# Hybrid conformer block: first gate pair's weight sums in the conv's spare buffers, token sums reordered, conv results in three places, fillers in two more attention slots

## The chip, the cores and the metric

The kernel runs on one core of one Trainium2 chip. The metric is the device time of one execution in microseconds; lower is better. Three runs of the kernel before took 1736.94, 1739.24 and 1739.51 us, a median of 1739.24.

## The reference

One transformer block over 1024 tokens with 1024 channels. `h @ w_in` gives five things: the two halves of a gated conv input, q, k and v for 16 heads, and the logits of two gates.

```python
h = rms_norm(x, norm1_g[l])
z = h @ w_in[l]
glu_in, q, k, v, gate_logits = jnp.split(z, SPLITS, axis=-1)
a = a_val * jax.nn.sigmoid(a_gate)
a = causal_depthwise_conv(a, conv_w[l], conv_b[l])      # width 31
a = jax.nn.silu(rms_norm(a, conv_norm_g[l]))
y_a = a @ w_conv_out[l]
...                                                     # dilated window attention, three groups
y_b = o @ w_attn_out[l]
g_a, g_b = jnp.split(jax.nn.sigmoid(gate_logits + gate_b[l]), 2, axis=-1)
x = x + (g_a * y_a + g_b * y_b) @ w_out[l]
h = rms_norm(x, norm2_g[l])
u = causal_depthwise_conv(h @ w_up[l], ffn_conv_w[l], ffn_conv_b[l])
x = x + (jax.nn.silu(u_gate) * u_val) @ w_down[l]
```

## The kernel before

All products run in fp32r with both operands split into a high part, rounded on ScalarE (ACT), and a low part, the difference, on VectorE (DVE). Three matmuls (high x high, high x low, low x high) make one product. `split` does the rounding and the difference; `wsplit` puts the two parts of a weight into the buffers `whi` and `wlo` (four each), and `stage` loads a weight or an activation block into one of four `raw` buffers of 128 x 1024 through the SP queue. Who wants a fifth `raw` buffer waits until the first is read for the last time.

The order of the stages: normed input; gated conv input; q, k, v; the gates; attention; the two output products; the feed-forward part. The 31-tap conv (`conv_branch`, L558) runs on VectorE beside the q, k, v products; its buffers are `cacc`, two of `codd` (513 columns), one `csum` (527 columns).

**The gate stage** computes 16 blocks of 128 gate channels for all 1024 tokens. Blocks 10 and 11 are plain products (`side_steps`, printed as `gate`). Ten others are done in five pairs (`PAIRS`, n = 0 to 4) by a Strassen-Winograd scheme: seven half-size products instead of eight. It needs sums of weight quarters (`sums`: s1 = g0 + g1, s2 = s1 - v0, s3 = v0 - g0, s4 = v1 - s2, four VectorE instructions of 128 x 512 on the pair's two raw weights v and g, with one more raw buffer for s1 and s2) and sums of token blocks. The token sums are made once, in `token_forms(i)` for i = 0 and 1, each for two of four k-blocks: it loads r22, r12, r11 into raw buffers and r21 into the place of its own result, forms three differences, and splits them into b12, t1 and t2; a fourth, t4, follows in the returned function `fourth`. The results lie in the pool `phT`, where the operands of the attention come later.

For each pair the loop (L805 on) runs the products in this order: X with s12 and t2, Y with s12 and t1, X with s3 and b12, then for n = 1 to 3 the first product of the next pair (`gx`), then X with s3 and t4 and Y with s4 (for n = 0 and 4 the other way round). Here X and Y are accumulators in PSUM; ScalarE and VectorE take them out as c11, c12, p5 and c21, which go to DRAM. `parts(n, which, name)` splits a weight sum, `load(n, which)` loads a weight.

**Interleaved with it:** `conv_factors` (n = 0) sums the conv's squares by matmul and takes the root on GpSimd; `conv_spread` (n = 1) builds a diagonal on VectorE and spreads it over the partitions by 16 matmuls (`psr`); `conv_result(c)` for c = 0 to 7 scales channel block c on VectorE, applies SiLU on ScalarE and stores it from ScalarE's queue. Blocks 0 to 3 stand in n = 1, 4 to 7 in n = 2, each time ahead of the b12 product.

**What sets the order.** Inside `tc.manual_schedule(engines=hand)` the instructions of ScalarE, VectorE and TensorE are issued as written. Everything else, such as the conv and all loads on the SP queue, is placed by a planner that works with estimated times; what is written earlier goes first where both could go. `tc.issue_after(ins)` keeps a block behind one instruction of the same engine. Each queue then runs in that fixed order.

**The attention** is a hand-ordered loop over 128 slots (head, half, query block): `score`, then `fill(front)`, the transposes `flip` of the slot five before, the weighted sums, `powers`, `share` and `fill(behind)`. `share` scales the probabilities on GpSimd. `fill(k)` takes k steps of three matmuls from the remaining plain gates and the conv's output product; `FRONT` and `BEHIND` give the numbers for the eight slots of a head. What is left of these steps runs after the last slot.

Of the kernel before, what the change touches and what calls it, by code (L numbers as in the profile page):

```python
# [13 lines left out]
F32 = mybir.dt.float32  # L14
F32R = mybir.dt.float32r
# [6 lines left out]
P = 128  # L22
# [13 lines left out]
FRONT = (1, 1, 0, 0, 0, 1, 0, 1)  # L36
BEHIND = (1, 1, 1, 1, 0, 1, 1, 0)
# [3 lines left out]
PAIRS = ((0, 1), (2, 3), (4, 5), (6, 7), (8, 9))  # L41
# [15 lines left out]
def block_kernel(ctx: ExitStack, tc: tile.TileContext, x, xT, x0, g2, pack, mask,  # L57
# [22 lines left out]
    def split(hi, lo, src):  # L80

        act.activation(hi, src, AF.Copy)  # L82
        dve.tensor_tensor(out=lo, in0=src, in1=hi.bitcast(F32), op=ALU.subtract)  # L83
# [216 lines left out]
    if True:  # L300
# [385 lines left out]
        def token_forms(i):  # L686
            ks = slice(2 * i, 2 * i + 2)
            view = lambda t: t.rearrange("p (a b) -> p a b", a=2)
            load = lambda n, k, half: stage(dh[:, k + 2 * i : k + 2 * i + 2, half * 512 : half * 512 + 512], f"h{n}_{i}")
            r22, r12, r11 = (view(load(n, k, half)) for n, k, half in (("22", 4, 1), ("12", 0, 1), ("11", 0, 0)))  # L690
            r21 = form["t4"][1][:, ks]
            sp.dma_start(r21.bitcast(F32), dh[:, 4 + 2 * i : 6 + 2 * i, 0:512])
            tt = lambda o, a, b, op: dve.tensor_tensor(out=o, in0=a, in1=b, op=op)
            tt(r11, r12, r11, sub)
            tt(r12, r22, r12, sub)
            tt(r22, r22, r11, sub)

            def rounded(dst, src):
                split(dst[0][:, ks], dst[1][:, ks], src)

            rounded(b12, r12)
            rounded(form["t1"], r11)
            rounded(form["t2"], r22)

            def fourth():
                tt(r22, r21.bitcast(F32), r22, sub)
                rounded(form["t4"], r22)

            return fourth

        def conv_factors():
            pss = bank_ps("pss")
# [47 lines left out]
        def load(n, which):  # L760
            raws[n][which] = stage(w_ch[16 + PAIRS[n][which]], f"g{which}_{n}")

        def sums(n):
            v, g = raws[n][0], raws[n][1]
            s = raws[n][2] = wp.tile([P, 1024], F32, tag="raw", bufs=4, name=f"gs_{n}")
            tt_(s[:, 0:512], g[:, 0:512], g[:, 512:], add)
            tt_(s[:, 512:], s[:, 0:512], v[:, 0:512], sub)
            tt_(g[:, 0:512], v[:, 0:512], g[:, 0:512], sub)
            tt_(v[:, 512:], v[:, 512:], s[:, 512:], sub)

        def parts(n, which, name):
            src = raws[n][which] if which != "s4" else raws[n][0][:, 512:]
            pw[n][name] = [four(t) for t in wsplit(src, f"{name}_{n}")]

        ENG = mybir.EngineType
        hand = {ENG.Activation, ENG.DVE, ENG.PE}
        with tc.manual_schedule(engines=hand):
            fourths = [token_forms(i) for i in range(2)]
            load(0, 0)
            load(0, 1)  # L780
            fourths[0]()
            sums(0)
            parts(0, 2, "s12")
            fourths[1]()
            parts(0, 1, "s3")
        with tc.issue_after(settled1.ins):
            conv_acc = conv_branch()
        cover(16 * len(PLAIN) - COVER)
        for _ in early_gates:
            pass  # L790
# [9 lines left out]
        with tc.manual_schedule(engines=hand):  # L800
            for n in range(2):
                xz[n] = gate_first(n, firsts[n])
                begun(n)
            load(1, 0)
            for n, (a, b) in enumerate(PAIRS):  # L805
                X = xz[n][:, 0:512]
                Y = bank_ps(f"gy_{n}")
                (sh, sl), (gh, gl) = pw[n]["s12"], pw[n]["s3"]
                inner = 0 < n < N - 1
                if n + 2 < N:  # L810
                    load(n + 2, 0)
                if n == 3:
                    p1_cm.__exit__(None, None, None)
                    p2_cm = tc.tile_pool(name="ph2", bufs=1, reuse_waits="tile")
                    p2 = p2_cm.__enter__()
                    pool2.append(p2)
                if n + 1 < N:
                    load(n + 1, 1)
                if n == 3:
                    tiles[0] = head(0)  # L820
                parts(n, "s4", "s4")
                if inner:
                    parts(n + 1, 0, "v")
                product(X, sh[:, 4:8], sl[:, 4:8], *form["t2"], False)
                c12 = quarter(f"c12_{n}")
                act.activation(c12, X, AF.Copy)
                product(Y, sh[:, 0:4], sl[:, 0:4], *form["t1"], True)
                p5 = quarter(f"p5_{n}")
                act.activation(p5, Y, AF.Copy)
                if n == 0:  # L830
                    rs8 = conv_factors()
                if n == 1:
                    conv_spread(rs8)
                if 0 < n < 3:
                    for c in range(4 * n - 4, 4 * n):
                        conv_result(c)
                product(X, gh[:, 0:4], gl[:, 0:4], *b12, False)
                tt_(p5, X, p5, add)
                sp.dma_start(dgate[b][:, 512:1024], p5)
                if n + 1 < N:  # L840
                    sums(n + 1)
                if inner:
                    xz[n + 1] = big_ps(f"gx_{n + 1}")
                    for i in range(2):
                        product(xz[n + 1][:, i * 512 : i * 512 + 512], *(t[:, 4 * i : 4 * i + 4] for t in pw[n + 1]["v"]),
                                *left[i], True)
                    parts(n + 1, 2, "s12")
                    begun(n + 1)
                else:
                    product(Y, *pw[n]["s4"], *b22, False)  # L850
                    tt_(c12, Y, c12, add)
                    if n + 1 < N:
                        parts(n + 1, 2, "s12")
                product(X, gh[:, 4:8], gl[:, 4:8], *form["t4"], False)
                c21 = quarter(f"c21_{n}")
                act.activation(c21, X, AF.Copy)
                sp.dma_start(dgate[b][:, 0:512], c21)
                if inner:
                    product(Y, *pw[n]["s4"], *b22, False)
# [12 lines left out]
    if True:  # L872
# [102 lines left out]
        with tc.manual_schedule(engines={ENG.Activation, ENG.DVE, ENG.PE}):  # L975
            pend = []
            fill(1)
            for at in range(len(slots) + BACK + 1):
                count[2] += 1
                cur = slots[at] if at < len(slots) else None  # L980
                front, behind = (FRONT[at % 8], BEHIND[at % 8] + (at == 4)) if cur else (2, 2)
                if cur is not None:
                    h, half, n = cur
                    if (half, n) == (0, 2) and h + 1 < H:
# [661 lines left out]
```

## Time and profile before

| what | value |
|---|---|
| median of three runs | 1739.24 us |
| profiled execution, whole | 1738.48 us |
| profiled execution, span from first to last instruction | 1736.5 us |
| granted TensorE clock over the span | 0.999 |
| TensorE busy | 99% of the span |
| VectorE busy | 77% of the span |
| ScalarE busy | 47% of the span |
| GpSimd busy | 10% of the span |

How to read the rows of the profile: PE is TensorE (PEld its weight loads), DVE VectorE, ACT ScalarE, POOL GpSimd, SP the queue that issues most transfers. Rows in order of time give the start in us from the span's start, the duration, the engine, the line of the kernel, the operation, what is written and read, and in brackets the idle time of that engine just before, with what ended it. Rows of waits give the engine and line that waited, what it waited for, the total, the number of times and the longest. The chain of waits is the work that ended last, followed back step by step.

### The profile page before, as it was taken

To read this page: it belongs to the slowest core of one execution; us is meant where nothing else is said; L and a number is where in the kernel's file an instruction comes from. 1 tells how busy PE (TensorE), PEld (TensorE's weight loads), DVE (VectorE), ACT (ScalarE), POOL (GpSimd) and SP (SyncE) were. 2 spreads that over 40 slices of the span, in tenths; PEclk is the share of its full clock that TensorE was granted. 3 is DMA by queue.
4 is the path that set the end of the run, shared out by engine and by line. 5 is a ranking of instruction groups with operands and counts; after the bars stand their busy time and mean duration, and the time that the engine had idled before them with its cause. 6 is when DMAs were issued, how large, how long until landed. Compare 5 with 4: busy or idle time off the path is not lost.

```text
span 1736.5 us, 22876 instructions
## 1 busy us (share of the span) xinstructions
PE 1725.9 (99%) x8147; PEld 1437.9 (83%) x8147; DVE 1333.1 (77%) x2032; ACT 810.7 (47%) x1284; POOL 178.6 (10%) x188
## 2 busy tenths in 40 slices
PE   9999999999999999999999999999999999999999
PEld 7888888888878888888888888888888888888887
DVE  5999999999776567867757663787777776789863
ACT  5421233233345577777765442555445444533431
POOL 0000232132000133332220000000000000000000
PEclk9999999999999999999999999999999999999999
DMA  9311145345537967877639585622221222398851
GB/s 375 139 53 49 51 140 170 109 134 176 180 122 240 291 185 216 238 216 201 198 122 338 206 296 203 225 107 85 86 85 73 85 85 85 128 370 307 292 176 49
DMA packets 159842, 299.02 MB, mean 172 GB/s; under 512 B 13296, under 2 KB 63088, under 8 KB 159216
## 3 DMA queue, kind: packets, MB, share of 16 engines
q1 hardware_dynamic: 157280, 291.14, 50.5%
q10 hardware_dynamic: 2448, 6.42, 0.9%
q8 instruction: 64, 1.05, 0.2%
q14 instruction: 50, 0.41, 0.1%
HBM read 213.62 MB, written 83.89 MB: 171 GB/s over the span
## 4 chain that ended last, share of the span: by engine, by line
PE 96%; DVE 1%; DMA 1%; issue 0%; ACT 0%; POOL 0%; SPq 0%; ACTq 0%; DVEq 0%; POOLq 0%
PE dx L1458 7%; PE xz L138 6%; PE xz L139 6%; PE xz L140 6%; PE dy L1458 5%; PE qkv L131 5%; PE qkv L133 5%; PE qkv L132 5%; PE pp L913 4%; PE y L138 2%; PE y L139 2%; PE y L140 2%; PE o L928 2%; PE o L927 2%; PE s L894 2%; PE s L893 2%
## 5 line engine op out<-in xcount | busy, mean ns | idle before, releaser
L131 PE MATMUL qkv<-hi_qkv,hT 128*128 128x512 f32 x384 | 151.2, 395 | 0.0
L133 PE MATMUL qkv<-hi_qkv,hT 128*128 128x512 f32 x384 | 149.8, 391 | 0.0
L132 PE MATMUL qkv<-lo_qkv,hT 128*128 128x512 f32 x384 | 149.8, 391 | 0.0
L83 DVE TENSOR_TENSOR pl<-pp,ph 128x512 fp32r<-128x512 f32 (+2 forms) x191 | 99.7, 550 | 42.4 <-ACT ph L82 42.0
L82 ACT ACTIVATE ph<-pp 128x512 fp32r<-128x512 f32 (+2 forms) x191 | 86.6, 489 | 74.0 <-PE pp L913 72.1
L898 DVE CUSTOM_DVE_ANT_0 p<-s,m 128x128 f32<-128x128 f32 (+3 forms) x120 | 90.5, 754 | 39.6 <-PE pp L913 22.0
L1361 DVE SCALAR_TENSOR_TENSOR u<-u,pk 128x1023 f32<-128x1023 f32 x88 | 112.4, 1279 | 1.2 <-ACT u L1359 0.9
L907 POOL TENSOR_SCALAR p<-p,st 128x128 f32<-128x128 f32 (+3 forms) x120 | 90.6, 756 | 206.0 <-DVE st L906 179.1
L107 POOL TENSOR_TENSOR rs<-ss,mhalf 128x8 f32<-128x8 f32 x32 | 69.5, 2175 | 291.4 <-DVE ss L106 291.3
L903 ACT ACTIVATE p<-p,st 128x128 f32<-128x128 f32 (+3 forms) x120 | 93.6, 780 | 8.2 <-DVE st L898 5.5
L580 DVE SCALAR_TENSOR_TENSOR cacc<-csum,both,cacc 128x512 f32<-128x512 f32 x120 | 90.0, 750 | 0.3
L580 DVE SCALAR_TENSOR_TENSOR cacc<-apad,pk,cacc 128x512 f32<-128x512 f32 x120 | 88.9, 751 | 0.0
L83 DVE TENSOR_TENSOR lo_uv<-raw_uv,hi_uv 128x1024 fp32r<-128x1024 f32 x20 | 24.5, 1226 | 79.9 <-ACT hi_uv L82 79.9
L580 DVE SCALAR_TENSOR_TENSOR codd<-apad,pk,codd 128x513 f32<-128x513 f32 x112 | 84.5, 755 | 0.7 <-ACT codd L573 0.7
L133 PEld LDWEIGHTS qkv<-hi_qkv,hT 128*128 128x128 f32 x384 | 72.1, 188 | 15.1
L132 PEld LDWEIGHTS qkv<-lo_qkv,hT 128*128 128x128 f32 x384 | 72.2, 188 | 14.2
L131 PEld LDWEIGHTS qkv<-hi_qkv,hT 128*128 128x128 f32 x384 | 72.1, 188 | 14.2
L913 PE MATMUL pp<-ident,p 128*128 128x128 f32 x540 | 79.8, 273 | 1.5 <-POOL p L907 1.4
L913 PEld LDWEIGHTS pp<-ident,p 128*128 128x128 f32 x540 | 64.1, 140 | 13.9 <-POOL p L907 2.4
L927 PE MATMUL o<-ph,v 128*128 128x512 f32 (+2 forms) x191 | 74.1, 392 | 0.0
L138 PE MATMUL xz<-blk_t,hi_s3g 128*128 128x512 f32 x176 | 68.7, 390 | 0.0
L138 PE MATMUL xz<-h2left,hi_uv 128*128 128x512 f32 x176 | 68.6, 390 | 0.0
(429 smaller groups left out, 4962.9 us busy)
## 6 DMA issues: line engine op xcount, KB each, us to landing
wr<-w_down SPq DMA_DIRECT2D x45, 512.0 KB, 5.5
gr<-dff SPq DMA_DIRECT2D x62, 256.0 KB, 5.0
raw_qkv<-w_qkv SPq DMA_DIRECT2D x24, 512.0 KB, 3.9
dff<-u SPq DMA_DIRECT2D x22, 512.0 KB, 2.6
raw_uv<-w_up SPq DMA_DIRECT2D x21, 512.0 KB, 3.2
raw_ug<-w_up SPq DMA_DIRECT2D x20, 512.0 KB, 3.2
raw_g<-w_ch SPq DMA_DIRECT2D x16, 512.0 KB, 4.0
dv<-v SPq DMA_DIRECT2D x16, 512.0 KB, 3.3
```

Source lines behind the costliest of these rows:

```text
L83: dve.tensor_tensor(out=lo, in0=src, in1=hi.bitcast(F32), op=ALU.subtract)
L131: pe.matmul(ps, ah, hi[:, k % 2, :], start=(k == 0), stop=False)
L132: pe.matmul(ps, ah, lo[:, k % 2, :], start=False, stop=False)
L133: pe.matmul(ps, al, hi[:, k % 2, :], start=False, stop=(k == KT - 1))
L138: pe.matmul(o, wh[:, k, :], bh[:, k, :], start=(start and k == 0), stop=False, skip_group_check=not start)
L139: pe.matmul(o, wh[:, k, :], bl[:, k, :], start=False, stop=False, skip_group_check=not start)
L140: end = pe.matmul(o, wl[:, k, :], bh[:, k, :], start=False, stop=(k == 3), skip_group_check=not start)
L580: dve.scalar_tensor_tensor(out=out_, in0=src[:, i : i + size], scalar=w(i), in1=out_, op0=ALU.mult, op1=ALU.add)
L913: pe.transpose(pp[:, qb * P : (qb + 1) * P], pts[qb][:, kt * P : (kt + 1) * P], ident)
L927: pe.matmul(o[:, c], v[:, kt, :], ph[:, c], start=(kt == 0), stop=False)
L1361: dve.scalar_tensor_tensor(out=acc[:, d:], in0=src[:, : T - d], scalar=w(2 - d), in1=acc[:, d:], op0=ALU.mult, op1=ALU.add)
L1458: pe.matmul(banks[n][:, cols], a[:, c], b[:, d], start=(start and i == 0 and m == 0), stop=(stop and i == nf - 1 and m == 2), skip_group_c ...
```

## The change

Five edits.

1. `token_forms` returns its three splits as functions, in the order t1, t2, b12, fourth, instead of running b12, t1, t2 at once. Step 0 runs b12, t1, t2 and its fourth. Step 1 runs t2, then the pair's weight sums and the split of s12, then t1, b12 and the split of s3. Its fourth moves into the pair loop, behind the split of s4 for n = 0.
2. The first pair's second weight is not loaded into a raw buffer but, in two halves of 256 KB, into the conv's `csum` buffer and into 512 new columns in the token pool. Its sums s1 and s2 go to the two `codd` buffers. `sums` and `parts` work on halves, so the splits of s12 and s3 of the first pair take two instructions of 512 columns on each engine instead of one of 1024.
3. `conv_branch` is written ahead of the token forms instead of behind them.
4. `conv_spread` moves behind the b12 product of n = 1. The conv's results 0 and 1 move to the end of n = 1, 2 to 5 stand in n = 2 ahead of the b12 product, 6 and 7 at the end of n = 2.
5. In slots 2 and 3 of the attention one more step is filled in (slot 4 already had one more).

```diff
             def rounded(dst, src):
-                split(dst[0][:, ks], dst[1][:, ks], src)
-
-            rounded(b12, r12)
-            rounded(form["t1"], r11)
-            rounded(form["t2"], r22)
+                return lambda: split(dst[0][:, ks], dst[1][:, ks], src)
 
             def fourth():
                 tt(r22, r21.bitcast(F32), r22, sub)
-                rounded(form["t4"], r22)
-
-            return fourth
+                rounded(form["t4"], r22)()
+
+            return rounded(form["t1"], r11), rounded(form["t2"], r22), rounded(b12, r12), fourth
...
         def sums(n):
-            v, g = raws[n][0], raws[n][1]
-            s = raws[n][2] = wp.tile([P, 1024], F32, tag="raw", bufs=4, name=f"gs_{n}")
-            tt_(s[:, 0:512], g[:, 0:512], g[:, 512:], add)
-            tt_(s[:, 512:], s[:, 0:512], v[:, 0:512], sub)
-            tt_(g[:, 0:512], v[:, 0:512], g[:, 0:512], sub)
-            tt_(v[:, 512:], v[:, 512:], s[:, 512:], sub)
+            (v0, v1), (g0, g1) = halves(raws[n][0]), halves(raws[n][1])
+            if 2 not in raws[n]:
+                raws[n][2] = wp.tile([P, 1024], F32, tag="raw", bufs=4, name=f"gs_{n}")
+            s0, s1 = halves(raws[n][2])
+            tt_(s0, g0, g1, add)
+            tt_(s1, s0, v0, sub)
+            tt_(g0, v0, g0, sub)
+            tt_(v1, v1, s1, sub)
...
         def parts(n, which, name):
-            src = raws[n][which] if which != "s4" else raws[n][0][:, 512:]
-            pw[n][name] = [four(t) for t in wsplit(src, f"{name}_{n}")]
+            src = raws[n][which] if which != "s4" else halves(raws[n][0])[1]
+            if isinstance(src, list):
+                hi, lo = (wp.tile([P, 1024], F32R, tag=f"w{a}", bufs=4, name=f"{a}_{name}_{n}") for a in ("hi", "lo"))
+                for c, t in zip(HALVES, src):
+                    split(hi[:, c], lo[:, c], t)
+                pw[n][name] = [four(t) for t in (hi, lo)]
+            else:
+                pw[n][name] = [four(t) for t in wsplit(src, f"{name}_{n}")]
...
+        with tc.issue_after(settled1.ins):
+            conv_acc = conv_branch()
+        raws[0][1] = [p1.tile([P, 527], F32, tag="csum", bufs=1, name="g1_0a")[:, 0:512], pT.tile([P, 512], F32, name="g1_0b")]
+        raws[0][2] = [p1.tile([P, 513], F32, tag="codd", bufs=2, name=f"gs_0{a}")[:, 0:512] for a in "ab"]
+        for i, t in enumerate(raws[0][1]):
+            sp.dma_start(four(t), w_ch[16 + PAIRS[0][1]][:, 4 * i : 4 * i + 4])
         with tc.manual_schedule(engines=hand):
-            fourths = [token_forms(i) for i in range(2)]
+            forms0 = token_forms(0)
+            for k in (2, 0, 1, 3):
+                forms0[k]()
+            first, second, third, fourth = token_forms(1)
             load(0, 0)
-            load(0, 1)
-            fourths[0]()
+            second()
             sums(0)
             parts(0, 2, "s12")
-            fourths[1]()
+            first()
+            third()
             parts(0, 1, "s3")
-        with tc.issue_after(settled1.ins):
-            conv_acc = conv_branch()
...
                 parts(n, "s4", "s4")
+                if n == 0:
+                    fourth()
...
+                if n == 2:
+                    for c in (2, 3, 4, 5):
+                        conv_result(c)
+                product(X, gh[:, 0:4], gl[:, 0:4], *b12, False)
                 if n == 1:
                     conv_spread(rs8)
-                if 0 < n < 3:
-                    for c in range(4 * n - 4, 4 * n):
-                        conv_result(c)
-                product(X, gh[:, 0:4], gl[:, 0:4], *b12, False)
...
                     begun(n + 1)
+                    for c in {1: (0, 1), 2: (6, 7)}.get(n, ()):
+                        conv_result(c)
...
-                front, behind = (FRONT[at % 8], BEHIND[at % 8] + (at == 4)) if cur else (2, 2)
+                front, behind = (FRONT[at % 8], BEHIND[at % 8] + (at in (2, 3, 4))) if cur else (2, 2)
```

More of the change, by code (lines that the diff above doesn't have):

```diff
@@ L761, in load, with halves @@
             raws[n][which] = stage(w_ch[16 + PAIRS[n][which]], f"g{which}_{n}")
+        def halves(t):
+            return t if isinstance(t, list) else [t[:, 0:512], t[:, 512:]]
         def sums(n):
-            v, g = raws[n][0], raws[n][1]
-            s = raws[n][2] = wp.tile([P, 1024], F32, tag="raw", bufs=4, name=f"gs_{n}")
-            tt_(s[:, 0:512], g[:, 0:512], g[:, 512:], add)
-            tt_(s[:, 512:], s[:, 0:512], v[:, 0:512], sub)
-            tt_(g[:, 0:512], v[:, 0:512], g[:, 0:512], sub)
```

## The prediction

> **What bounds the kernel now.** I read the page first, then the list of waits of the matmul engine, then that engine in order of time, and then the chain of work around the one long wait.
>
> ```profile
> span 1736.5 us, 22876 instructions
> PE 1725.9 (99%) x8147; PEld 1437.9 (83%) x8147; DVE 1333.1 (77%) x2032; ACT 810.7 (47%) x1284; POOL 178.6 (10%) x188
> ```
>
> TensorE is busy for 1725.9 of 1736.5 us, and no matmul is added or removed by the change. So it can win only where TensorE stands or runs slowly. Its waits, over the whole span (total, times, longest):
>
> ```profile
> PE gx L138 <- ACT hi_s L82: 2.2, 1, 2.2
> ...
> PE pp L913 <- POOL p_first L907: 0.7, 1, 0.7
> PE gx L140 <- DVE lo_s L83: 0.5, 1, 0.5
> PE psr L727 <- DVE dgs L722: 0.3, 1, 0.3
> ```
>
> The change aims at these four: the two of gx (first gate pair), psr (the conv's factors spread) and p_first (the attention's first flip). The first pair's place in order of time (start, duration, what it waited for):
>
> ```profile
> 478.97 0.39 PE L138 MATMUL gx<-hT,hi_gw 128*128 128x512 f32 x1
> ...
> 489.62 0.39 PE L140 MATMUL gx<-hT,lo_gw 128*128 128x512 f32 x1
> 492.25 0.50 PE L138 MATMUL gx<-gt,hi_s 128*128 128x512 f32 x1 [2.25 <-ACT hi_s L82]
> ...
> 493.51 0.80 PE L140 MATMUL gx<-gt,lo_s 128*128 128x512 f32 x1 [0.53 <-DVE lo_s L83]
> 494.11 0.63 PE L138 MATMUL gx<-gt,hi_s 128*128 128x512 f32 x1
> 494.53 0.63 PE L139 MATMUL gx<-gt,hi_s 128*128 128x512 f32 x1
> ...
> 497.24 0.39 PE L138 MATMUL gy<-gt,hi_s 128*128 128x512 f32 x1
> ```
>
> From 478.97 to 489.62 lie 47 steps: one matmul every 0.2266 us. After 489.62, 13 steps lead to the first gy at 497.24. At that pace it would start at 489.62 + 13 x 0.2266 = 492.57. So this place costs 4.67 us, of which only 2.78 is shown as idle: after the wait the matmuls come every 0.42 us (494.11 to 494.53), and the clock row says why (columns: length, busy time of PE, PEld, DVE, ACT and POOL, granted clock, DMA share, GB/s):
>
> ```profile
> 490.00:500.00 10.00, 7.23 (x27) 5.57 (x26) 8.12 (x10) 4.67 (x6) 0.00 (x0) 0.83 0.47 171
> ```
>
> [...]
>
> **What makes it late.** The chain of waits before it:
>
> ```profile
> 464.76 5.80 DMA gt<-dh
> 470.56 1.22 DVE hT L83
> 471.77 1.14 DVE gt L83
> 472.94 5.49 DMA raw_h<-dh
> 478.55 1.24 DVE raw_h L693
> ...
> 485.70 1.14 DVE raw_h L693
> ...
> 486.87 1.07 ACT gt L82
> ...
> 489.70 0.69 DVE gs L758
> ...
> 491.11 1.20 DVE raw_g L758 x2
> ```
>
> and the loads on the SP queue, with a row of the page for how long such a weight load takes to land (4.0 us):
>
> ```profile
> 455.31 4.02 SPq L87 DMA_DIRECT2D raw_h<-dh  x3
> ...
> 471.80 1.49 SPq L87 DMA_DIRECT2D raw_h<-dh  x2
> ...
> 483.45 0.34 SPq L87 DMA_DIRECT2D raw_g<-w_ch  x1
> ```
> ```profile
> raw_g<-w_ch SPq DMA_DIRECT2D x16, 512.0 KB, 4.0
> ```
>
> Only four raw buffers exist. The token blocks of step 0 hold them until 471.8, those of step 1 follow, and the pair's weight loads get a buffer only from 483.45 on. The second lands near 489, the four weight sums run from 489.70, and TensorE's second wait, for the low half of their split, ends at 493.51. TensorE wanted it at 489.85.
>
> **The change, part by part.**
>
> **The first pair's second weight and its sums leave the raw buffers.** They go into the conv's csum and codd buffers and 2 KB of the token pool, so its load can be issued as soon as the conv's last squares are added, which the trace has at:
>
> ```profile
> 468.21 0.69 DVE L591 TENSOR_TENSOR sqacc<-sqacc,csum 128x512 f32<-128x512 f32 x1
> ```
>
> It lands by about 468.9 + 4 = 473. The first weight needs the raw buffer of step 0's r22, which the new order frees early: `fourth` of step 0 (now 485.70: a subtraction of 1.14, a copy of 1.07 on ACT and a split of 1.14, some 3.4 us) comes straight after the third split of step 0, in VectorE's idle time ahead of 478.55, where step 1's blocks land. The three splits of step 0 end at 470.56 + 3 x 1.14 = 474.0, so it ends at about 477.4, and the weight lands at 477.4 + 4.0 = 481.4. The blocks of step 1 still arrive at 478.4, since their buffers come free at the same two splits. Then VectorE does, in the new order: three block sums of 1.24 to 482.2; the t2 split (ACT 1.07, then 1.14) to 484.5; four weight sums of 0.60 to 486.9; the s12 split in two halves of 0.6 to 488.1. **So TensorE finds both operands 1.7 us before 489.85.** Next it needs t1 (at 489.85 + 12 x 0.2266 = 492.57; split ends 489.3), then b12 and s3 (after gy and the conv's sum of squares, past 496; ends 490.4 and 491.6), then the step-1 `fourth`, moved behind s4, past 500 (ends 495.6). None is late. All of the 4.67 us is counted, for the clock never falls if TensorE never stands. From below: if the step-1 blocks and weights land 3 us later, which is a doubling of half their flight, 1.3 us of wait stay, and with the slow steps behind them some 2.
>
> The conv is now traced ahead of the token forms, so its last six VectorE instructions may go before them instead of between them. That is 0 to 2.4 us (four at 0.6) earlier for the forms, since VectorE waits for step 0's blocks anyway. I take 0.
>
> **The next deadline.** Behind this stands the second pair's split:
>
> ```profile
> 508.53 1.22 DVE L83 TENSOR_TENSOR lo_s<-gs,hi_s 128x1024 fp32r<-128x1024 f32 x1
> ```
> ```profile
> 509.96 0.39 PE L138 MATMUL gx<-gt,hi_s 128*128 128x512 f32 x1
> ```
>
> It ends at 509.75, 0.2 us before it is read. It starts from TensorE's own product b12, so it moves with TensorE, as long as its weights are there. These take raw buffers freed by t1, b12 and s4 of the first pair (489.3 to 492.2), land by 496.2 and are needed near 499.9. I take 0; if they kept their old times, this would give back 1 to 2 us.
>
> **The spread of the conv's factors** goes behind the product b12. It costs TensorE the step from 515.17 to 515.89, of 0.72 instead of 0.23: 0.49 us.
>
> ```profile
> 515.17 0.39 PE L140 MATMUL gy<-gt,lo_s 128*128 128x512 f32 x1
> 515.89 2.05 PE L727 MATMUL psr<-dgs,ones 128*128 128x128 f32 x16 [0.33 <-DVE dgs L722]
> ```
>
> With 12 matmuls (2.72 us) between, the diagonals are done before TensorE asks: all 0.49 us is won. The p5 sum and the third pair's sums queue behind the two copies of psr on VectorE, but four conv products (4.6 us) no longer stand before them, so they come earlier.
>
> **The conv's results** keep their eight products and eight SiLUs. Two go to the end of n=1, four stay in n=2, two go to the end of n=2. The last two come ahead of the s3 split of the fourth pair:
>
> ```profile
> 518.71 4.63 DVE L733 TENSOR_TENSOR cacc<-cacc,sqacc 128x1024 f32<-128x1024 f32 x4
> ```
> ```profile
> 549.52 1.23 DVE L83 TENSOR_TENSOR lo_s<-raw_g,hi_s 128x1024 fp32r<-128x1024 f32 x1 [2.46 <-ACT hi_s L82]
> ```
> ```profile
> 555.91 0.39 PE L138 MATMUL gx<-hT,hi_s 128*128 128x512 f32 x1
> ```
>
> Two products of 1.16 and two SiLUs, taken by the ACT row of that size above, 1.07, push that split by 4.5 us at most, if nothing overlaps: from 550.75 to 555.2. It is read at 555.91: covered, and taken as 0.
>
> **Two more fillers** (the sum over slots 2, 3, 4 is three; slot 4 had one already). Each is three matmuls, 0.68 us, moved from the attention's end to its start. The place they fill:
>
> ```profile
> 592.57 0.49 PE L913 MATMUL pp<-ident,p_first 128*128 128x128 f32 x3
> 593.75 0.33 PE L913 MATMUL pp<-ident,p_first 128*128 128x128 f32 x1 [0.70 <-POOL p_first L907]
> ```
> ```profile
> 592.65 1.05 POOL L907 TENSOR_SCALAR p_first<-p_first,st 128x512 f32<-128x512 f32 x1 [0.46 <-DVE st L906]
> ```
>
> GpSimd's share ends at 593.70; its chain hangs on VectorE and ACT, not on the fillers. TensorE comes 1.36 us later to the flip, past 593.70: the 0.70 us is won. At the end two steps fewer cover the first weights of the next stage:
>
> ```profile
> 920.93 3.49 DVE L83 TENSOR_TENSOR lo_ao<-raw_ao,hi_ao 128x1024 fp32r<-128x1024 f32 x3
> ```
> ```profile
> 922.82 0.39 PE L114 MATMUL yb<-oT,hi_ao 128*128 128x512 f32 x1
> ```
>
> The first of the three is done at 922.1; the first yb would stand at 921.46 and read it two steps later, 921.9. I charge 0.3 us (0 to 0.7).
>
> **Sum:** 4.67 + 0.49 + 0.70 - 0.30 = 5.56 us. The profiled execution took 1738.48 us (span 1736.5 and 2.0 around it): 1732.9. The median of the runs, 1739.24, stands 0.76 above it: **1733.7 us**. Its own range is 1732.2 to 1735.5.
>
> **The rivals.**
>
> *Half of it comes back.* The freed time meets the next deadlines: late weights of the second pair (1 to 2 us), or a rest of the wait in the first (2 us). For it: 0.2 us of margin at 509.75. Against it: all loads are triggered earlier. 5.56 - 2.5 = 3.1 won: 1736.2.
>
> *The loads of the first pair block the SP queue.* SP's rows come one after another, so one that waits holds those behind it. If the csum load is placed ahead of the three raw_h loads at 455.31, these wait for the conv's release at 468.9 instead. They then land at about 475, step 0 (three sums, three splits, the fourth: 10.3 us) ends at 485.8; step 1's blocks, freed at 480 to 481, land at 486.8; and the chain worked out above (9.6 us from there) ends at 496.1. TensorE stands 6.25 us instead of 2.78, and with the same 1.9 us of slow steps the place costs 8.15: 3.5 more than now, less 0.9 from the other parts: 1741.8, slower. The three loads are issued by 455.31 + 4.02 = 459.3 now and the chain has 1.7 us to spare, so it decides from about 461 on, and each further microsecond costs one. For it: the load is traced first. Against it: a load is placed when its buffer is expected free, and VectorE's order has that behind the first block sum, which itself needs those three loads.
>
> *The change doesn't do what it says.* The instructions of the conv and the forms land on VectorE in another order than traced, the s12 split stays near 493, and only psr and p_first are won: 1739.24 - 0.9 = 1738.3.
>
> **How the numbers follow.** Forecast 0.60; half back 0.17; blocked queue 0.13; not as said 0.10. A measurement of this kernel tells about 0.2% from no change, 3.5 us: faster means under 1735.8, slower over 1742.7. The forecast is faster nearly throughout (0.58), half back in four tenths of its cases (0.07); the blocked queue is slower by that much where it is held past 470 (0.07, and 0.03 for a mishap of it elsewhere). Faster 0.65, same 0.25, slower 0.10. The range runs from 1731.8 (the forms 2.4 us earlier bring nothing, but the attention's start up to 1 us more, and no charge at its end) to 1740.0, which holds all but the blocked queue.
>
> **What would show it.** Right: no wait of gx on hi_s or lo_s, a granted clock of 1.00 through the first pair, the first gy some 4.7 us earlier; `fourth` of step 0 before step 1's block sums; psr without a wait; no p_first wait of the flip, and a wait of at most 0.7 us at the first yb. Wrong: raw_h loads issued after 460; a new wait of gx near the second pair; a stand at pp after the fillers. The forecast falls if TensorE's waits over the span still sum to more than 5 us.

## The result, and the profile after

| | median | lowest to highest | runs |
|---|---|---|---|
| before | 1736.94 us | 1735.88 to 1739.51 | 7 |
| after | 1731.92 us | 1731.03 to 1732.61 | 7 |

The ratio is 0.9967 (95% interval 0.9956 to 0.9979): 5.0 us faster by the medians. The forecast of 1733.7 us lies 1.8 us above the time measured; its own range (1732.2 to 1735.5) missed it by 0.3 us, the wide range (1731.8 to 1740.0) holds it at its lower edge. Seven runs of the kernel before put its median at 1736.94, 2.3 us below that of the three shown ahead of the prediction.

The profiled execution after took 1731.03 us. The page:

```profile
span 1729.2 us, 22890 instructions
...
PE 1724.0 (100%) x8147; PEld 1438.0 (83%) x8147; DVE 1334.7 (77%) x2034; ACT 810.2 (47%) x1286; POOL 175.5 (10%) x188
```

TensorE's waits of the kernel after, all that the view lists (total, times, longest):

```profile
PE early L461 <- POOL ones L340: 1.0, 1, 1.0
PE pp L931 <- POOL p_first L925: 0.4, 1, 0.4
PE s L911 <- DVE st_first L916: 0.2, 1, 0.2
PE pp L931 <- POOL p L925: 0.2, 1, 0.2
```

Both waits of gx and the one of psr are gone. So is the wait of 0.7 us at the flip of the fourth share, but one of 0.4 us stands at a later flip (597.89). TensorE's waits in the attention are named by the share on GpSimd (L925; L907 before).

The first pair, after, in order of time: the SP queue, then VectorE, then TensorE.

```profile
455.06 4.02 SPq L87 DMA_DIRECT2D raw_h<-dh  x3
...
468.24 0.35 SPq L789 DMA_DIRECT2D g_0a<-w_ch  x1
...
471.11 1.50 SPq L87 DMA_DIRECT2D raw_h<-dh  x2
...
476.99 0.34 SPq L87 DMA_DIRECT2D raw_g<-w_ch  x1
```
```profile
473.39 1.23 DVE L693 TENSOR_TENSOR raw_h<-gt,raw_h 128x1024 f32<-128x1024 f32 x1
...
476.88 3.74 DVE L693 TENSOR_TENSOR raw_h<-raw_h,raw_h 128x1024 f32<-128x1024 f32 x3
...
482.89 0.69 DVE L754 TENSOR_TENSOR gs_0a<-g_0a,g_0b 128x512 f32<-128x512 f32 x1
...
486.62 0.68 DVE L83 TENSOR_TENSOR lo_s<-gs_0b,hi_s 128x512 fp32r<-128x512 f32 x1
```
```profile
489.37 0.39 PE L140 MATMUL gx<-hT,lo_gw 128*128 128x512 f32 x1
...
490.05 0.39 PE L140 MATMUL gx<-gt,lo_s 128*128 128x512 f32 x1
...
492.31 0.39 PE L138 MATMUL gy<-gt,hi_s 128*128 128x512 f32 x1
```

The half that the csum buffer takes is asked for at 468.24, the first weight at 476.99 instead of after 483. Step 0's fourth runs at 473.39 in the gap that VectorE used to wait out, the weight sums start at 482.89 instead of 489.70, and the split of s12 ends at 487.30. TensorE reads its low half first at 490.05, 2.7 us later. By the prediction's formula the place costs 492.31 - 489.37 - 13 x 0.2266 = 0.0 us. The granted clock stays whole (the row of the windows, columns as before):

```profile
490.00:500.00 10.00, 10.00 (x53) 8.54 (x53) 4.64 (x8) 3.10 (x5) 1.64 (x1) 1.00 0.53 176
```

Between the two profiled executions the span fell by 7.3 us, not by the sum's 5.56. Part by part, by how far the same matmuls have moved against each other: first pair 4.7, psr 0.6, the attention's first flips 0.3, **the slots between 670 and 710 us 1.3**, the end of the attention -0.4. The rest, 0.8 us in pieces of at most 0.3, lies at the start of the kernel and in later stages, where the change touches nothing. The 1.3 us was not in the sum. Its row stood in the list of waits of the kernel before, and the prediction left it out (two of the three waits, 0.81 and 0.31 us, lie at 681.40 and 701.63, the third at 859.14):

```profile
PE pp L913 <- POOL p L907: 1.4, 3, 0.8
```

### The profile page after: what moved, and what is told of

It is laid out like the page before. It is cut to its first block, busy times and chain, and to the rows that moved or that the text cites. A ratio compares the mean times of both kernels' runs of the same rounds, so it can differ in the third digit from the quotient of the medians.

```text
span 1729.2 us, 22890 instructions
## 1 busy us (share of the span) xinstructions
PE 1724.0 (100%) x8147; PEld 1438.0 (83%) x8147; DVE 1334.7 (77%) x2034; ACT 810.2 (47%) x1286; POOL 175.5 (10%) x188
## 4 chain that ended last, share of the span: by engine, by line
PE 94%; DMA 3%; DVE 1%; ACT 1%; issue 1%; SPq 0%; ACTq 0%; POOL 0%; DVEq 0%
PE dx L1476 7%; PE xz L138 6%; PE xz L139 6%; PE xz L140 6%; PE dy L1476 5%; PE qkv L133 5%; PE qkv L131 5%; PE qkv L132 5%; PE pp L931 4%; PE y L139 2%; PE y L138 2%; PE y L140 2%; PE o L946 2%; PE s L912 2%; PE s L911 2%; PE o L945 2%
## 5 line engine op out<-in xcount | busy, mean ns | idle before, releaser
L925 POOL TENSOR_SCALAR p<-p,st 128x128 f32<-128x128 f32 (+3 forms) x120 | 90.6, 756 | 204.4 <-DVE st L924 174.2
L132 PEld LDWEIGHTS qkv<-lo_qkv,hT 128*128 128x128 f32 x384 | 72.2, 188 | 14.3
```

Source lines behind the costliest of these rows:

```text
L132: pe.matmul(ps, ah, lo[:, k % 2, :], start=False, stop=False)
```

## The experiments

Each run is held against runs of the kernel before on the same chip. Those gave medians of 1737.56 us (26 runs), 1736.95 (25) and 1736.71 (16) in the three sets below, and 1734.85 to 1740.91 in all: a spread of 6 us.

**First set: the parts alone.** The fillers alone, on the kernel before:

```diff
-                front, behind = (FRONT[at % 8], BEHIND[at % 8] + (at == 4)) if cur else (2, 2)
+                front, behind = (FRONT[at % 8], BEHIND[at % 8] + (at in (2, 3, 4))) if cur else (2, 2)
```

> The kernel before with the two more fillers alone. Theory A (each edit works at its own place): the flip's wait at the attention's start shrinks by 0.3 to 0.7 us, the two waits of pp near 681 and 701 (2.1 us of lost steps in the profile of before, 0.7 in that of after) go because the weight splits come two steps earlier, and the first yb loses 0.4: 1.2 to 1.5 us faster than before in all. Theory B (the waits near 681 and 701 are scatter between executions of the kernel before): they stay in this profile, and the time is within 0.4 us of before.

Measured: 1737.38 us (1735.20 to 1739.61, 11 runs), ratio 0.9999 (0.9990 to 1.0008). The interval is 3 us wide, so it says nothing of an effect below 1 us. The waits of its profiled execution say more. They read, of the attention:

```profile
PE yb L114 <- DVE gg L1068: 0.6, 1, 0.6
...
PE pp L913 <- POOL p L907: 0.5, 2, 0.3
PE pp L913 <- POOL p_first L907: 0.4, 1, 0.4
```

The waits for the share go from 2.1 us (1.4 and 0.7) to 0.9, and a new one of 0.6 stands at yb. What remains, 0.6 us, is too little for this measurement.

The reverse, the kernel after without the two extra fillers:

```diff
-                front, behind = (FRONT[at % 8], BEHIND[at % 8] + (at in (2, 3, 4))) if cur else (2, 2)
+                front, behind = (FRONT[at % 8], BEHIND[at % 8] + (at == 4)) if cur else (2, 2)
```

> The changed kernel without the two more fillers. Theory A: 1.2 to 1.5 us slower than the changed kernel, with pp waits of about 0.7 at the first flip and about 1 us near 676 and 696 back. Theory B: within 0.4 us of the changed kernel, 5 to 5.5 us faster than before.

Measured: 1732.55 us (1731.88 to 1734.09, 8 runs), ratio 0.9970 (0.9960 to 0.9980). It is repeated in the third set beside the changed kernel.

Edits 1 to 3 alone (the forms, the spare buffers and the conv written first; the conv's results and the fillers as before):

```diff
-                if n == 2:
-                    for c in (2, 3, 4, 5):
-                        conv_result(c)
+                if n == 1:
+                    conv_spread(rs8)
+                if 0 < n < 3:
+                    for c in range(4 * n - 4, 4 * n):
+                        conv_result(c)
                 product(X, gh[:, 0:4], gl[:, 0:4], *b12, False)
-                if n == 1:
-                    conv_spread(rs8)
...
-                    for c in {1: (0, 1), 2: (6, 7)}.get(n, ()):
-                        conv_result(c)
...
-                front, behind = (FRONT[at % 8], BEHIND[at % 8] + (at in (2, 3, 4))) if cur else (2, 2)
+                front, behind = (FRONT[at % 8], BEHIND[at % 8] + (at == 4)) if cur else (2, 2)
```

> Edits 1 to 3 alone: the first pair's sums in the conv's buffers and the token sums in order of need; conv results and fillers as before. Theory A: the 4.7 us of the first pair go and nothing else, so 4.4 to 4.9 us faster than before; psr keeps its wait of 0.3 us. Rival (half of it comes back at the second pair's split, which has 0.2 us to spare): 2 to 3 us faster, with a wait of gx at n = 1.

Measured: 1732.82 us (1732.43 to 1733.72, 7 runs), ratio 0.9971 (0.9960 to 0.9983). These three edits carry nearly all of the win, and with them the spread falls from 6 us to 1.3. So the spread of the kernel before comes mostly from the place that they mend.

Edit 4 alone, on the kernel before (the same lines the other way round):

> Edit 4 alone: conv_spread behind the b12 product, the conv's results in three places. Theory A: 0.5 to 0.6 us faster than before, psr without a wait, nothing lost later. Rival: the results 6 and 7 ahead of the fourth pair's split make gx wait at n = 3, so no gain or a loss of up to 0.5.

Measured: 1737.91 us (1735.58 to 1740.21, 11 runs), ratio 0.9999 (0.9990 to 1.0007): lost in the spread. In its profile psr starts without a wait. What the run teaches stands in its first pair, which it doesn't touch; the matmuls and the clock there:

```profile
490.26 0.39 PE L140 MATMUL gx<-hT,lo_gw 128*128 128x512 f32 x1
493.22 0.50 PE L138 MATMUL gx<-gt,hi_s 128*128 128x512 f32 x1 [2.57 <-ACT hi_s L82]
...
494.48 0.50 PE L140 MATMUL gx<-gt,lo_s 128*128 128x512 f32 x1 [0.53 <-DVE lo_s L83]
...
496.89 0.39 PE L138 MATMUL gy<-gt,hi_s 128*128 128x512 f32 x1
```
```profile
490.00:495.00 5.00, 1.90 (x7) 0.95 (x6) 4.80 (x7) 1.55 (x2) 0.00 (x0) 1.00 0.14 53
495.00:500.00 5.00, 5.00 (x26) 4.15 (x25) 4.13 (x5) 3.20 (x5) 0.00 (x0) 1.00 0.66 217
```

TensorE stands longer than in the profile of before (3.10 us against 2.78), yet the clock does not fall, and the place costs 496.89 - 490.26 - 2.95 = 3.7 us instead of 4.7 (2.95 is 13 x 0.2266). So even without a fall of the clock the first steps behind the waits cost 0.6 us beyond the idle time; with it they cost 1.9. The chain of waits of the same execution has the three transfers behind it:

```profile
465.40 6.04 DMA gt<-dh
...
473.82 5.33 DMA raw_h<-dh
...
485.66 4.91 DMA raw_g<-w_ch
```

**Second set: the halves of the first pair's edit, the blocked queue, and before once more.** The new order of work with the old buffers (the second weight and the sums in raw buffers, both loads behind the token work):

```diff
-        raws[0][1] = [p1.tile([P, 527], F32, tag="csum", bufs=1, name="g1_0a")[:, 0:512], pT.tile([P, 512], F32, name="g1_0b")]
...
-            load(0, 0)
             second()
-            sums(0)
-            parts(0, 2, "s12")
             first()
             third()
+            load(0, 0)
+            load(0, 1)
+            sums(0)
+            parts(0, 2, "s12")
             parts(0, 1, "s3")
```

> The changed kernel with the first pair's weights and sums back in the raw buffers (the early fourth of step 0, the late fourth of step 1 and all other edits kept; step 1's three splits come ahead of the weight sums, since they must free the buffers). Theory A (the raw buffers bind): the second weight is issued only behind step 1's t1 split, at about 486, lands at 490, and the sums end as late as before: gx waits 2 to 3 us again, and the time is 0 to 1.5 us below that of before. Rival (the order of the token sums alone is what helps): no wait of gx, 4.5 us or more below before.

Measured: 1734.98 us (1734.07 to 1737.98, 10 runs), ratio 0.9990 (0.9980 to 0.9999). The second weight has to wait for a raw buffer, lands late, and one wait stays (the SP queue and TensorE):

```profile
476.67 0.34 SPq L87 DMA_DIRECT2D raw_g<-w_ch  x1
...
483.81 0.33 SPq L87 DMA_DIRECT2D raw_g<-w_ch  x1
```
```profile
490.94 0.50 PE L140 MATMUL gx<-gt,lo_s 128*128 128x512 f32 x1 [0.53 <-DVE lo_s L83]
```

The place costs 1.1 us here; the wait of gx is shorter than the 2 to 3 us that were expected, and the time is 2.0 us below before instead of 0 to 1.5. The same profile has a new wait of 0.5 at the plain gates (`gate` for `hi_gt`); the rest of its distance to the changed kernel was not traced further.

The spare buffers with the old order of work (b12, t1, t2 for both steps, then the fourths around the sums):

```diff
-            forms0 = token_forms(0)
-            for k in (2, 0, 1, 3):
-                forms0[k]()
-            first, second, third, fourth = token_forms(1)
+            fourths = []
+            for i in range(2):
+                first, second, third, fourth = token_forms(i)
+                third()
+                first()
+                second()
+                fourths.append(fourth)
             load(0, 0)
-            second()
+            fourths[0]()
             sums(0)
             parts(0, 2, "s12")
-            first()
-            third()
+            fourths[1]()
...
-                if n == 0:
-                    fourth()
```

> The changed kernel with the old order of the token sums, and the second weight and the sums in the spare buffers. The first weight then gets its raw buffer at about 483 as before and lands at 487.5, and fourth of step 0 stands ahead of the sums on VectorE until 489: the s12 split ends near 492.5. Theory A: gx waits 1.5 to 2.5 us, and the time is 1 to 2.5 us below before. Rival (the buffers alone are enough): no wait, as fast as the changed kernel.

Measured: 1734.35 us (1732.82 to 1737.09, 10 runs), ratio 0.9986 (0.9977 to 0.9995). That is 2.6 us below before. In the profile the place costs 1.9 us; TensorE's two waits:

```profile
491.38 0.50 PE L138 MATMUL gx<-gt,hi_s 128*128 128x512 f32 x1 [0.32 <-ACT hi_s L82]
...
493.13 0.50 PE L140 MATMUL gx<-gt,lo_s 128*128 128x512 f32 x1 [1.01 <-DVE lo_s L83]
```

So neither half suffices: in its one profile each leaves 1 to 2 us at this place, and each leaves a spread of some 4 us. Only with both is there time to spare.

The prediction's rival of the other sign, brought about by an edit: step 0's token blocks are issued behind the csum load on the SP queue.

```diff
+            held = sp.dma_start(four(t), w_ch[16 + PAIRS[0][1]][:, 4 * i : 4 * i + 4])
+            if i == 0:
+                csum_load = held
...
-            forms0 = token_forms(0)
+            with tc.issue_after(csum_load.ins):
+                forms0 = token_forms(0)
```

> The changed kernel with the token blocks of step 0 queued on SP behind the load into the conv's csum buffer: the mishap of the second rival, made on purpose. By the prediction's price the loads start at 468 to 469 instead of 455, gx stands about 6 us, and the place costs 8 us: 1739 to 1741 us, 7 to 9 above the changed kernel. Rival (VectorE, free of the token sums, ends the conv some 3 us sooner, so that the load is issued near 465): 4 to 5 us of cost, 1736 to 1737 us.

Measured: 1741.75 us (1739.98 to 1743.37, 10 runs), ratio 1.0021 (1.0012 to 1.0031): slower. The SP queue, TensorE, and the windows:

```profile
465.69 0.33 SPq L789 DMA_DIRECT2D g_0a<-w_ch  x1
466.07 3.56 SPq L87 DMA_DIRECT2D raw_h<-dh  x3
```
```profile
489.69 0.39 PE L140 MATMUL gx<-hT,lo_gw 128*128 128x512 f32 x1
494.34 0.60 PE L138 MATMUL gx<-gt,hi_s 128*128 128x512 f32 x1 [4.27 <-ACT hi_s L82]
...
500.52 0.63 PE L138 MATMUL gy<-gt,hi_s 128*128 128x512 f32 x1
```
```profile
490.00:500.00 10.00, 5.01 (x12) 3.44 (x12) 9.40 (x13) 5.76 (x9) 0.00 (x0) 0.73 0.25 80
```

The blocks leave 11 us later, and the place costs 500.52 - 489.69 - 2.95 = 7.9 us up to the first gy, with the next matmul still slow (0.63). The prediction had put that price at 8.15, with a wait of 6.25 us and 1.9 us of slow steps. Here the waits are 4.99 us, and 2.9 us are lost in slow steps. The median lies 9.8 us above that of the changed kernel, more than the 7 to 9 expected. The changed kernel itself, with raw_h at 455.06, stays clear of it.

The kernel before once more, for a second draw of its first pair:

> The kernel before once more, for another profile of the first pair's place. The runs of before fall into two groups, 1736.0 to 1736.8 and 1738.3 to 1740.9 us. Theory C (the clock's fall after the wait, which the profile of before shows and two of the four profiles since do not, makes the upper group): a time near 1736.5 goes with steps of 0.23 us behind the wait and a place that costs 2 to 3 us, a time near 1739 with steps of 0.43 us and 4.5 to 5 us. Rival (the groups come from elsewhere, such as the attention's waits): the place costs the same in both, and the difference shows at 670 to 710.

Measured: 1735.13 us. TensorE, and the transfers of its chain of waits:

```profile
489.04 0.39 PE L140 MATMUL gx<-hT,lo_gw 128*128 128x512 f32 x1
489.94 0.50 PE L138 MATMUL gx<-gt,hi_s 128*128 128x512 f32 x1 [0.52 <-ACT hi_s L82]
...
491.20 0.50 PE L140 MATMUL gx<-gt,lo_s 128*128 128x512 f32 x1 [0.53 <-DVE lo_s L83]
...
493.60 0.39 PE L138 MATMUL gy<-gt,hi_s 128*128 128x512 f32 x1
```
```profile
464.18 4.90 DMA gt<-dh
...
471.45 4.64 DMA raw_h<-dh
...
482.61 4.13 DMA raw_g<-w_ch
```

The same code costs 493.60 - 489.04 - 2.95 = 1.6 us here. The three transfers took 13.7 us together, against 16.3 in the profile of edit 4 alone: 2.6 us less, and the two waits are 2.05 us shorter. In the profile of the fillers alone they took 14.3 us, and the waits were 1.67 us. Four profiled executions have the old code at this place: cost 1.6 with a time of 1735.13, 2.2 with 1735.84 (the fillers alone), 3.7 with 1738.11 (edit 4 alone), 4.7 with 1738.48 (the first profile). Time less cost is 1733.5, 1733.6, 1734.4 and 1733.8. The step from cost to time is rough, for two of the four carry another edit elsewhere, worth 1.2 us (the fillers) and 0.3 to 0.6 us (edit 4) by the runs of this record. The granted clocks of the runs say more. Of the 67 runs of the kernel before in the three sets, 37 have a mean clock of 1.000 over their span and a median of 1736.29 us; 30 have 0.999 or 0.998, a median of 1738.59 us, and none of them is under 1737.40. All 49 runs of the changed kernel and of the versions whose profile has no wait of gx have 1.000. In the first profile of before the windows show where the clock falls: it is 0.50 from 493.0 to 496.4 us, and 1.00 on either side. **So the upper group of the old code's times is, with little overlap, the runs in which the clock fell.** Where it fell the record shows for the profiled runs alone; the two with a mean below 1.000 (before, and the blocked queue) have the fall at this place (0.83 and 0.73 from 490 to 500 us). The fall itself costs some 1.3 us of the 2.3 between the groups (1.9 us of slow steps against 0.6); that the rest is the length of the waits, by the flight of transfers, is not shown.

**Third set: beside the changed kernel itself.** The changed kernel again, unedited:

> The changed kernel itself, for the three beside it. Theory: no wait at the first gate pair, so nothing that differs from one execution to the next there; 1731.0 to 1732.6 us again, a spread of under 2 us, while the kernel before spreads over 4 to 6 us. Rival: its narrow spread was luck, and some executions come above 1734.

Measured: 1731.70 us (1730.74 to 1731.91, 5 runs), ratio 0.9968 (0.9956 to 0.9981). With the seven runs of the result, twelve lie within 1.9 us.

Without the two extra fillers, once more:

> The changed kernel once more without its two extra fillers, beside the changed kernel itself on the same chip. Theory: the fillers are worth about 1.0 us in the slots around 670 to 710 us (where the scaled probabilities of the share are waited for), 0.4 us at 580 to 610, and cost 0.5 us at the end of the attention; so this is 0.6 to 0.9 us slower than the changed kernel. Rival, the prediction's own sum (0.70 won, 0.30 paid): 0.4 us slower, and nothing at 670 to 710.

Measured: 1732.87 us (1732.17 to 1734.37, 8 runs), ratio 0.9979 (0.9969 to 0.9989). All eight runs lie above all five of the changed kernel; the medians are 1.2 us apart, where the prediction's sum had 0.4. TensorE's flips stand at the fourth share (0.65 us), as the prediction had it, and again 88 us later. At that later place, first without and then with the fillers:

```profile
676.51 0.77 PE L931 MATMUL pp<-ident,p 128*128 128x128 f32 x5 [0.81 <-POOL p L925]
```
```profile
676.51 0.77 PE L931 MATMUL pp<-ident,p 128*128 128x128 f32 x5 [0.15 <-POOL p L925]
```

Both go on at 676.51, when the share is done. With the fillers TensorE comes 0.66 us later to the same work, and the share does not; had it moved with TensorE, the wait would have stayed. What makes it late without the fillers is a split of the conv output's weight (lo_co) on VectorE, ahead of the powers of a short slot; GpSimd idles 0.99 us for it:

```profile
672.97 1.42 DVE L179 TENSOR_TENSOR lo_co<-raw_co,hi_co 128x512 fp32r<-128x512 f32 x1
```
```profile
674.84 1.97 POOL L925 TENSOR_SCALAR p<-p,st 128x1024 f32<-128x1024 f32 x2 [0.99 <-DVE st L924]
```

With the fillers that split and the next one stand at 666.03 and 668.85, and this share follows the one before it without idle time. At the flip of 597.89 it is the other way round. GpSimd there, first without and then with the fillers, and VectorE with them:

```profile
595.91 1.13 POOL L925 TENSOR_SCALAR p_first<-p_first,st 128x1024 f32<-128x1024 f32 x1 [0.38 <-DVE st L924]
```
```profile
596.71 1.12 POOL L925 TENSOR_SCALAR p_first<-p_first,st 128x1024 f32<-128x1024 f32 x1 [0.91 <-DVE st L924]
```
```profile
594.93 1.40 DVE L179 TENSOR_TENSOR lo_gt<-raw_gt,hi_gt 128x512 fp32r<-128x512 f32 x1
```

The scores of TensorE just there lie within 0.04 us of each other in the two kernels. With the fillers a split of a gate's weight (lo_gt) has come ahead of the powers; without them it stands behind, at 596.54. So the fillers change when the weights are split that they read, and by this the later shares, for better or worse.

One filler more, in slot 7:

```diff
-                front, behind = (FRONT[at % 8], BEHIND[at % 8] + (at in (2, 3, 4))) if cur else (2, 2)
+                front, behind = (FRONT[at % 8], BEHIND[at % 8] + (at in (2, 3, 4, 7))) if cur else (2, 2)
```

> The changed kernel with one filler more, in slot 7 of the attention: three matmuls moved once more from the attention's end to the flip that still waits 0.4 us for the share at about 598. Theory: up to 0.5 us won there, 0.2 to 0.5 paid at the end, where the first product of the next stage already stands for its low weights: within 0.4 us of the changed kernel either way. Rival: the end has slack again, and it is 0.5 us faster.

Measured: 1731.47 us (1731.04 to 1732.19, 6 runs), ratio 0.9969 (0.9957 to 0.9981), not told apart from the changed kernel. The wait at 598 is gone, and another has come up at 717, with the same three rows of VectorE, GpSimd and TensorE as at 676 without the fillers:

```profile
714.11 1.42 DVE L179 TENSOR_TENSOR lo_co<-raw_co,hi_co 128x512 fp32r<-128x512 f32 x1
```
```profile
715.98 1.97 POOL L925 TENSOR_SCALAR p<-p,st 128x1024 f32<-128x1024 f32 x2 [0.99 <-DVE st L924]
```
```profile
717.65 0.77 PE L931 MATMUL pp<-ident,p 128*128 128x128 f32 x5 [0.81 <-POOL p L925]
```

The number of fillers decides into which slot such a split falls.

The changed kernel with the conv's spread and results at their old places (edit 4 undone, lines as above):

> The changed kernel with the conv's spread and its eight results back at their old places (four in n = 1, four in n = 2). Theory, from the prediction: TensorE stands again at psr, 0.5 to 0.6 us slower than the changed kernel, and nothing else moves. Rival: the four conv products ahead of the spread also hold back the third pair's sums, and it is over 1.5 us slower.

Measured: 1732.29 us (1731.32 to 1733.28, 8 runs), ratio 0.9972 (0.9962 to 0.9982): 0.6 us above the changed kernel beside it, with overlapping runs. psr stands again, as in the kernel before (the changed kernel's list of waits above has none there):

```profile
512.33 2.05 PE L723 MATMUL psr<-dgs,ones 128*128 128x128 f32 x16 [0.33 <-DVE dgs L718]
```

No version beat the changed kernel by more than the runs can tell.

## Why the prediction was right, and where it was wrong

**The chain of the first pair: right, within about 1 us at each step.** The csum half was put after 468.2 (468.24), the first weight at 477.4 (476.99), the end of the s12 split at 488.1 (487.30), and no wait, a whole clock and the first gy 4.7 us earlier followed. That the conv traced first shifts nothing was right too. The "from below" case, a rest of the wait, did not come: there are 2.7 us to spare.

**"All of the 4.67 us is counted": right for that execution, wrong for the median.** The step took the cost of one execution as the cost of the kernel. It was the dearest of four draws (1.6 to 4.7, mean 3.1), and one with a fall of the clock, which 30 of 67 runs have. The base went the same way: the three runs had a median of 1739.24, but the kernel's is near 1737. Taking 4.67 from a profile of 1738.48 was consistent in itself. Taken as a gain over the median, it is not: by the medians, edits 1 to 3 bring 4.7 us against the 26 runs beside them, and some 3.2 when the third set's 1736.71 is taken and the fillers and the conv, 1.2 and 0.6 us, are counted off from its 5.0.

**The slow steps behind the wait, counted in full: too strong.** The row with 0.83 shows one fall of the clock, behind a wait of 2.25 us. Behind one of 2.57 us, in another execution, there was none (1.00 over the same 10 us), and behind one of 4.27 us there was one again (0.73). That such a wait always brings the slow steps was the author's estimate from one execution, and what sets the moment of a fall no run here shows. Of the 1.9 us of slow steps, 1.3 should have been a term that is there in some executions only; 0.6 stand behind the waits with a whole clock too. The other side of the step, "the clock never falls if TensorE never stands", is borne out as far as the runs go: the 49 runs of the changed kernel and of the versions without a wait of gx have a mean clock of 1.000, with other waits of up to 1.0 us in the profile of the changed kernel.

**The fillers: the step that was mis-sized.** "The 0.70 us is won", less 0.30, made 0.40; the run without them gives 1.2. At its own flip the wait did go, but 0.4 us came back at 597.89, where the kernels without extra fillers have none. "Its chain hangs on VectorE and ACT, not on the fillers" is what failed there: the chain does hang on VectorE, but VectorE also splits the weights that the fillers read, and two fillers more put such a split (lo_gt, 1.40 us) ahead of the powers. Then 1.3 us came back between 670 and 710, at waits for the share (0.81 and 0.31 us) that were in the list and that the prediction did not read, since "the change aims at these four"; there the split of lo_co had stood in the way and no longer does. The prediction foresaw neither, so the gain beyond its 0.40 is luck.

**The charge at the attention's end**, 0.3 us (0 to 0.7): the wait at yb was 0.2 to 0.6 us in five profiles of other versions with the fillers, 0.3 in one without them (edits 1 to 3 alone), and under what the view lists in both profiles of the changed kernel. It lies in the bounds and varies.

**psr:** 0.49 expected; 0.6 by the shift of the matmuls and by the medians of the third set, 0.3 by those of the first (1732.82 without edit 4, 1732.55 with it). **The next deadlines:** the second pair's split moved forward with TensorE and made no new wait, as taken; nor did the conv's results 6 and 7 ahead of the fourth pair's split.

**The rivals.** *Half comes back* did not happen. *The blocked queue* did not arise: raw_h was issued at 455.06, far from 461. Brought about by an edit, the csum load left at 465.69 and raw_h right behind it at 466.07, in the order that the prediction took; it cost 7.9 us against 8.15, and the time was 1741.75 against 1741.8, but both agree in part by luck. The wait was 1.3 us shorter and the slow steps 1.0 us longer than taken, and the time was counted from 1739.24, 2.3 us above the median measured here. The working also has small slips (475 + 10.3 is 485.3, not 485.8; 486.8 + 9.6 is 496.4, not 496.1). *Not as it says* falls with the first fence.

The forecast came out 1.8 us high because the span of the profiled execution fell by 7.3 us and not by 5.56. The 1.3 us at 670 to 710 were not in the sum, 0.8 us lie where the change touches nothing, and the fillers' own flip and the end brought 0.5 less, psr 0.1 more. The lower end of the wide range is no better founded: 1733.7 less the 1.0 and 0.3 that it names is 1732.4, not 1731.8, so that it holds 1731.92 is luck. Two sizes were off in opposite ways: the typical cost of the first pair was taken too high, the fillers too low. With about 3.1 + 0.6 + 1.2 the gain would be 4.9 us, and 5.0 was measured; these terms were put together afterwards, and the 3.1 rests on four draws.

What stays open: why the transfers of the first pair take 13.7 us in one execution and 16.3 in another, and what exactly makes the clock fall. Only four profiles show the old code there; of the other runs the record has the time and the mean clock alone.

## What to carry to other kernels

The cost of a wait in one profile is one draw (here 1.6 to 4.7 us in four). Where the chain behind it holds transfers, look at a second and a third execution before it is entered in a sum, and take the base from enough runs; a mend that leaves a margin of some us (here 2.7) takes away the spread together with the mean (here from 6 us to 1.9). Read every row of the list of waits that the change could reach, also those at which it does not aim: work moved on one engine also moves the preparation that it triggers on another, here the splits of the weights on VectorE, and with it waits far behind.

## What the runs showed of the hardware

The flight of one 512 KB transfer of token blocks, on the chain of waits, was 4.64 us in two executions and 5.33 and 5.49 in two others of like code; that of gt ran from 4.90 to 6.04. In one execution TensorE's granted clock fell to 0.50 at 493.0 us, behind a wait of 2.25 us that ended at 492.25, and stayed there until 496.4 (3.4 us; 0.83 over 10 us). In another it stayed at 1.00 from 490 to 500 us, behind a wait of 2.57 us, so the length of the wait alone did not decide between these two. In a third, behind a wait of 4.27 us that ended at 494.34, it was 0.73 from 490 to 500 us and 0.93 from 500 to 510; at 0.50 that makes some 6.8 us, from about 494.6 to 501.4. At a clock of 0.50 the matmuls of 128 x 512 came every 0.43 us, at 1.00 every 0.23.
